# Five of eleven down-projection chunks as seven block products, their weight sums on GpSimd, and the splits at the stage ends placed otherwise

## The chip, the cores and the metric

The kernel runs on one core of a Trainium2 chip. The number that counts is the device time of one execution in microseconds (us). A core has a matrix engine (TensorE, PE in the rows; its weight loads are PEld), a vector engine (VectorE, DVE), an engine for activations and copies (ScalarE, ACT), a general engine (GpSimd, POOL) and an engine that issues transfers (SyncE, SP). Each works through its own program in order and waits on semaphores of the others. Matmuls write to PSUM, eight banks of 128x512 numbers; everything else lies in SBUF.

## The reference

Two layers, each with a feed-forward network, a token mixer and a second feed-forward network, on 256 tokens of 1024 numbers, all in fp32:

```python
def swiglu(h, w_gate_up, w_down):
    gu = h @ w_gate_up                      # 1024 -> 2 * 2816
    g, u = jnp.split(gu, 2, axis=-1)
    return (jax.nn.silu(g) * u) @ w_down    # 2816 -> 1024

for l in range(2):
    x = x + 0.5 * rms_norm(swiglu(rms_norm(x, ffn1_pre[l]), ...), ffn1_post[l])
    x = x + rms_norm(hybrid_mixer(rms_norm(x, mix_pre[l]), ...), mix_post[l])
    x = x + 0.5 * rms_norm(swiglu(rms_norm(x, ffn2_pre[l]), ...), ffn2_post[l])
```

The change touches the product with `w_down`, of which there are four, and the passage from each of them to what follows.

## The kernel before

Every product is made in three passes. A number is split into hi, its value in the matrix engine's fp32r form, and lo, the rest; a product is then hi by hi, hi by lo and lo by hi. Weights come from memory raw, in chunks of 128x2048 (two transfers of 512 KB into two `raw` tiles). ACT casts a raw half to hi, DVE subtracts hi from raw and writes lo. PE uses both.

**Feeding.** `stream` is the list of all chunks in the order of use. `issue` starts a chunk's two transfers and puts the steps of its split into the list `parts`; `part` takes steps off it and writes them into the engines' programs. ACT, DVE and PE keep the order in which they were written (`InOrder`). There are five buffers of hi and of lo (`LOOK + 1`), and six `raw` tiles. `chunk` hands out the next chunk and, through `top_up`, issues as many more as the five buffers hold.

**Block chunks.** In a down projection a chunk is 256 rows of `w_down` by 1024 columns, used with two blocks of 128 tokens. A plain chunk costs 24 matmuls of 512 columns. For the chunks in `FAST` the chunk is taken as two by two blocks of weights (b11, b12, b21, b22, each 128x512) and the activations likewise, and the product is made from seven block products instead of eight (`seven`, with `PRODUCTS`): 7 times three passes, 21 matmuls. The sums of activation blocks that this needs are made in `forms`. The sums of weight blocks are made in place in the raw tiles by four additions of 128x512 (`add`, lines 162 to 172), on DVE. A block chunk so has seven blocks to split and occupies two of the five buffers (`t` with b11, b21, b22; `t2` with four sums). Its steps are, in the order of `parts`: hi of b11; hi of b21 and b22; lo of b11; two additions; hi of the first two sums; lo of b21 and b22; two additions; hi of the last two sums; lo of the four sums. Additions overwrite what earlier steps read, and the last hi needs all four.

**A down projection.** `DOWN` is the order of its eleven chunks. Seven block products use seven PSUM banks; after the last block chunk, `combine` adds the extra banks into the four output banks (DVE, five operations, then three more), while PE does the chunk behind it, the joining chunk. The last three chunks (`TAIL`) are done for the first 128 tokens and then for the second. After the first block `on_block` runs `post` (norm of the result, added to x) and `pre` (norm for the next stage, tile `xn`), PE turns `xn` (`turn`), and then the same for the second block. The next stage begins in `fill` with four chunks.

**Around it.** In the gate and up products before a down projection, ACT copies PSUM banks and DVE adds them (`add_up`), between the splits that `part` puts there. GpSimd has the power of the norms (line 263) and some memsets only.

Of the kernel before, what the change touches and what calls it, by code (L numbers as in the profile page):

```python
# [10 lines left out]
F32 = mybir.dt.float32  # L11
F32R = mybir.dt.float32r
# [4 lines left out]
P = 128  # L17
T = 256
D = 1024
# [14 lines left out]
WARM = 16  # L34
TURN0 = (9, 11)

DOWN = (2, 0, 4, 1, 6, 3, 8, 5, 7, 9, 10)
FAST = (2, 4, 6, 8)


PRODUCTS = (
# [24 lines left out]
@with_exitstack  # L66
def trunk(ctx: ExitStack, tc: tile.TileContext, x, gains, gcol, feat, wgu1, wd1, win, wco, wpg, wpo, wo, wgu2, wd2, out):
    nc = tc.nc
    pe, act, dve = (InOrder(tc, e) for e in (nc.tensor, nc.scalar, nc.vector))
    const = ctx.enter_context(tc.tile_pool(name="const", bufs=1))  # L70
    raws = ctx.enter_context(tc.tile_pool(name="raws", bufs=6))
    whi = ctx.enter_context(tc.tile_pool(name="whi", bufs=LOOK + 1))
# [4 lines left out]
    wide = ctx.enter_context(tc.tile_pool(name="wide", bufs=1))  # L77
# [7 lines left out]
    HALF = (slice(0, 512), slice(512, 1024))  # L85
# [41 lines left out]
    def issue(now=True):  # L127

        i = state["issued"]
        state["issued"] = i + 1  # L130
        name, l, c = stream[i]
        h = CHUNK // 2
        raw = []
        for s in range(2):
            raw.append(raws.tile([P, h], F32, name="raw"))
            nc.sync.dma_start(raw[s], src[name][l, c, :, s * h : (s + 1) * h])
        new = lambda: (whi.tile([P, CHUNK], F32R, name="hi"), wlo.tile([P, CHUNK], F32R, name="lo"))

        def hi(t, at, n, r, off):
            parts.append(lambda: act.copy(t[0][:, at : at + n], raw[r][:, off : off + n]))  # L140

        def lo(t, at, n, r, off):
            parts.append(
                lambda: dve.tensor_tensor(
                    t[1][:, at : at + n], raw[r][:, off : off + n], t[0][:, at : at + n].bitcast(F32), op=ALU.subtract
                )
            )

        t = new()
        if cost(i) == 1:  # L150
            for s in range(2):
                hi(t, s * h, h, s, 0)
                lo(t, s * h, h, s, 0)
            ready[i] = t
        else:


            t2 = new()
            q = h // 2
            b12, b11 = raw[0][:, :q], raw[0][:, q:]  # L160
            b21, b22 = raw[1][:, :q], raw[1][:, q:]
            add = lambda o, x, y, op: parts.append(lambda: dve.tensor_tensor(o, x, y, op=op))
            upper, lower = (t, 0, q, 0, q), (t, q, h, 1, 0)
            hi(*upper)
            hi(*lower)
            lo(*upper)
            add(b11, b11, b12, ALU.subtract)
            add(b12, b22, b12, ALU.subtract)
            hi(t2, 0, h, 0, 0)
            lo(*lower)  # L170
            add(b22, b22, b11, ALU.add)
            add(b21, b21, b22, ALU.subtract)
            hi(t2, h, h, 1, 0)
            lo(t2, 0, h, 0, 0)
            lo(t2, h, h, 1, 0)
            ready[i] = t + t2
        if now:
            part(len(parts))
# [3 lines left out]
    def part(n=1):  # L182
        for _ in range(n):
            if parts:
                parts.pop(0)()
# [70 lines left out]
    def rstd(parts, scale):  # L256

        v0 = small.tile([P, 1], F32, name="v0")
        dve.tensor_scalar(v0, parts[0], scale / D, scale * EPS, op0=ALU.mult, op1=ALU.add)
        v1 = small.tile([P, 1], F32, name="v1")  # L260
        dve.tensor_scalar(v1, parts[1], scale / D, v0, op0=ALU.mult, op1=ALU.add)
        r = small.tile([P, 1], F32, name="r")
        nc.gpsimd.tensor_tensor(r, v1, mhalf, op=ALU.pow)  # L263
        return r

    def sumsq(src_half):
        junk = tmp.tile([P, 512], BF16, name="junk", bufs=1)
        s = small.tile([P, 1], F32, name="ss", bufs=8)
        act.activation(junk, src_half, AF.Square, accum_out=s)
        return s  # L270

    def post(b, banks, gain, scale):

        mul = lambda s: dve.tensor_tensor(banks[s], banks[s], gain[:, HALF[s]], op=ALU.mult)
        ss = sumsq(banks[0])
        mul(0)
        s1 = sumsq(banks[1])
        if b:
            part()
        r = rstd([ss, s1], scale)  # L280
        mul(1)
        for s in range(2):
            dve.scalar_tensor_tensor(
                xs[b][:, HALF[s]], banks[s], r, xs[b][:, HALF[s]], op0=ALU.mult, op1=ALU.add
            )
        if b:
            part()

    def pre(b, gain, r=None):

        if r is None:
            r = rstd([sumsq(xs[b][:, HALF[s]]) for s in range(2)], 1.0)
        xn = wide.tile([P, D], F32, name="xn")
        for s in range(2):
            dve.scalar_tensor_tensor(
                xn[:, HALF[s]], xs[b][:, HALF[s]], r, gain[s], op0=ALU.mult, op1=ALU.mult
            )
        return xn
# [27 lines left out]
    def act_slot(dtype=F32):  # L326

        return acts.tile([P, 2, 512], dtype, name="act", tag="act")
# [4 lines left out]
        split((t[:, :, 0, :], t[:, :, 1, :]), src_ap, 1)  # L333
        return [(t[:, i], t[:, i, 0, :], t[:, i, 1, :]) for i in range(2)]

    def forms(h):


        a = h.rearrange("p i (b t) -> p (i b) t", b=NB)
        sums = tmp.tile([P, 2, T + 2], F32, name="sums", tag="cu", bufs=1)  # L340
        sums = sums.rearrange("p i t -> p (i t)")[:, : 4 * P].rearrange("p (i t) -> p i t", t=P)
        dve.tensor_tensor(sums[:, 0], a[:, 0], a[:, 2], op=ALU.add)
        dve.tensor_tensor(sums[:, 1], sums[:, 0], a[:, 1], op=ALU.subtract)
        dve.tensor_tensor(sums[:, 2], a[:, 1], a[:, 0], op=ALU.subtract)
        dve.tensor_tensor(sums[:, 3], a[:, 3], sums[:, 1], op=ALU.subtract)
        fh, fl = (act_slot(F32R).rearrange("p i (x t) -> p (i x) t", t=P) for _ in range(2))
        split((fh[:, 0:3], fl[:, 0:3]), a[:, 1:4], 1)
        split((fh[:, 3:7], fl[:, 3:7]), sums, 1)
        return fh, fl


    def out_product(name, order, acts_hl, on_block, fast={}):
# [40 lines left out]
        def combine():  # L393

            new = lambda tag: tmp.tile([P, 2, T], F32, name=tag).rearrange("p i t -> p (i t)")
            p1 = new("sil")
            act.copy(p1, extra[1])
            u2 = new("h")
            dve.tensor_tensor(u2, extra[6], p1, op=ALU.add)
            u3 = new("h")  # L400
            dve.tensor_tensor(u3, extra[7], u2, op=ALU.add)
            yield 0, 0
            dve.tensor_tensor(banks[0][0], banks[0][0], u3, op=ALU.add)
            dve.tensor_tensor(u3, u3, extra[5], op=ALU.subtract)
            yield 0, 1
            dve.tensor_tensor(banks[0][1], banks[0][1], u3, op=ALU.add)
            yield 1, 0
            top_up(1)
            dve.tensor_tensor(banks[1][0], banks[1][0], p1, op=ALU.add)
            dve.tensor_tensor(u2, u2, extra[5], op=ALU.subtract)  # L410
            yield 1, 1
            dve.tensor_tensor(banks[1][1], banks[1][1], u2, op=ALU.add)
# [20 lines left out]
        for h in range(2):  # L433
            for c in range(TAIL):
                if len(ws) <= c:
                    ws.append(chunk(name, c))
                for kk in range(2):
                    step(0, h, order[nchunk - TAIL + c], ws[c], kk)
        on_block(0, banks[0])
# [49 lines left out]
    def ffn(l, gu, dn, acts_hl, on_block, gains_):  # L489
        slot = act_slot()  # L490
        tok = [slot[:, f, :] for f in range(2)]

        def take(b, f, p):
            sil = tmp.tile([P, CC], F32, name="sil")
            act.activation(sil, p[:, :CC], AF.Silu)
            dve.tensor_tensor(tok[f][:, b * CC : (b + 1) * CC], p[:, CC:], sil, op=ALU.mult)

        fill(gu, acts_hl, take)
        hs, fast = [], {}
        for f in range(2, NFU):  # L500
            ps = feat_product(gu, acts_hl)
            if f == 2:
                hs += split_pair(turn_back(tok[0]))
            sil = add_up(ps, "sil")
            act.activation(sil, sil, AF.Silu)
            ps = feat_product(gu, acts_hl)
            if f == 2:
                hs += split_pair(turn_back(tok[1]))
            h = add_up(ps, "h")
            dve.tensor_tensor(h, h, sil, op=ALU.mult)  # L510
            if f in FAST:
                fast[f] = forms(h)
                hs += [None, None]
            else:
                hs += split_pair(h)
        gains_()
        out_product(dn, DOWN, hs, on_block, fast)

# [124 lines left out]

    def scaled(b, r):

        xn = wide.tile([P, D], F32, name="xn")
        for h in HALF:
            dve.tensor_scalar(xn[:, h], xs[b][:, h], r, None, op0=ALU.mult)
        return xn
# [114 lines left out]
```

## Time and profile before

| | |
|---|---|
| median of 3 runs | 1172.24 us (1172.19 to 1172.38) |
| profiled execution, its own time | 1171.4 us |
| its span, first to last instruction | 1169.6 us |
| PE busy | 1155.9 us, 99% |
| DVE busy | 914.2 us, 78% |
| ACT busy | 674.1 us, 58% |
| GpSimd busy | 17.3 us, 1% |
| granted TensorE clock, mean | 0.999 |

A profile has a page of totals and several views of the trace behind it. The busy share says how much an engine works, the timeline what ran when and what ended an engine's idle time (in brackets), and the chain of waits which work, followed back from the end, had nothing to spare. A matmul's end is modelled and overlaps the next one's start, so its pace is read from starts. Operations on one engine overlap a little as well; the time after which the next one starts is called the pitch below.

### The profile page before, as it was taken

The numbers are of one execution on the slowest core, as the hardware profiler recorded it, in microseconds if no ns is written. First come the engines' busy times: TensorE is split into PE (matmuls) and PEld (weight loads), VectorE is DVE, ScalarE is ACT, GpSimd is POOL, SyncE is SP. The second block draws the span as 40 slices with busy tenths as digits, with TensorE's granted clock in tenths as the row PEclk, the third lists the DMA queues.
The fourth block names the chain that finished last, engine by engine and source line by source line (L and its number), as shares of the span: only waits on it lengthen the run. The fifth ranks groups of instructions, "written<-read, shape, count | busy, mean of one in ns | idle before, by whom it ended". The sixth has DMA issues, their size and how long they took to land.

```text
span 1169.6 us, 16393 instructions
## 1 busy us (share of the span) xinstructions
PE 1155.9 (99%) x6144; PEld 991.8 (85%) x6144; DVE 914.2 (78%) x1301; ACT 674.1 (58%) x1042; POOL 17.3 (1%) x75
## 2 busy tenths in 40 slices
PE   8999999999999999999999999999999999999997
PEld 5888888888898888888788888878888988888885
DVE  6777798587988767769986769976789786777795
ACT  7565465655565566655565555656556565565561
POOL 0000000000000000000000000000000000000000
PEclk9999999999999999999999999999999999999999
DMA  9665366655466574636765554765565655565361
GB/s 323 223 207 184 108 231 222 230 182 188 157 210 201 173 259 159 201 109 200 267 209 189 182 178 142 244 210 204 183 202 193 191 187 172 201 199 195 126 196 56
DMA packets 62575, 225.00 MB, mean 192 GB/s; under 512 B 7328, under 2 KB 7328, under 8 KB 62496
## 3 DMA queue, kind: packets, MB, share of 16 engines
q1 hardware_dynamic: 62352, 223.96, 57.4%
q8 instruction: 48, 0.79, 0.3%
q14 instruction: 31, 0.25, 0.1%
q10 hardware_dynamic: 144, 0.00, 0.0%
HBM read 222.88 MB, written 1.05 MB: 191 GB/s over the span
## 4 chain that ended last, share of the span: by engine, by line
PE 78%; DVE 14%; DMA 3%; issue 2%; ACT 2%; POOL 0%; DVEq 0%; POOLq 0%; ACTq 0%
PE ps L63 78%; DVE lo L63 8%; DVE raw L63 3%; DMA raw<-in_wd 2%; DMA raw<-in_win 1%; DVE h L63 1%; ACT hi L63 1%; DMA raw<-in_wgu 0%; POOL r L263 0%; ACT junk L63 0%; ACT act L63 0%; DVE ps L63 0%; DVE x L63 0%; DVE xn L63 0%; DVE act L63 0%
## 5 line engine op out<-in xcount | busy, mean ns | idle before, releaser
L63 DVE TENSOR_TENSOR lo<-raw,hi 128x1024 fp32r<-128x1024 f32 (+1 forms) x444 | 522.9, 1201 | 37.1 <-ACT hi L63 36.5
L63 ACT CAST hi<-raw 128x1024 fp32r<-128x1024 f32 (+1 forms) x444 | 448.9, 1034 | 80.5 <-DVE raw L63 55.3
L63 PE MATMUL ps<-xt,hi 128*128 128x512 f32 x1792 | 419.0, 390 | 0.0
L63 PEld LDWEIGHTS ps<-xt,hi 128*128 128x128 f32 x1792 | 332.6, 188 | 66.6
L63 PE MATMUL ps<-hi,act 128*128 128x512 f32 x800 | 235.5, 391 | 0.2
L63 PEld LDWEIGHTS ps<-xt,lo 128*128 128x128 f32 x1792 | 222.7, 192 | 4.4
L63 PE MATMUL ps<-xt,lo 128*128 128x256 f32 x1792 | 225.1, 283 | 0.0
L63 PEld LDWEIGHTS ps<-hi,act 128*128 128x128 f32 x800 | 149.9, 188 | 32.4 <-DVE h L63 1.9
L63 PE MATMUL ps<-lo,act 128*128 128x512 f32 x400 | 140.4, 390 | 0.9 <-DVE lo L63 0.9
L63 DVE TENSOR_TENSOR h<-ps,h 128x256 f32<-128x256 f32 (+1 forms) x140 | 58.6, 430 | 79.4 <-ACT h L63 79.2
L63 ACT COPY h<-ps 128x256 f32<-128x256 f32 x136 | 49.2, 373 | 122.7 <-PE ps L63 122.7
L63 PE MATMUL ps<-hi,xt 128*128 128x512 f32 x384 | 99.8, 394 | 1.0 <-ACT hi L63 0.9
L63 PEld LDWEIGHTS ps<-lo,act 128*128 128x128 f32 x400 | 75.1, 188 | 17.0 <-DVE lo L63 1.7
L63 PEld LDWEIGHTS ps<-hi,xt 128*128 128x128 f32 x384 | 71.1, 188 | 16.0 <-ACT hi L63 1.3
L63 ACT COPY sil<-ps 128x256 f32<-128x256 f32 (+1 forms) x124 | 45.6, 382 | 67.2 <-PE ps L63 67.2
L63 ACT CAST act<-h 128x512 fp32r<-128x512 f32 (+1 forms) x60 | 35.6, 593 | 69.5 <-DVE h L63 69.5
L63 PE MATMUL ps<-act,hi 128*128 128x512 f32 (+1 forms) x320 | 71.4, 369 | 0.0
L63 PEld LDWEIGHTS ps<-act,hi 128*128 128x128 f32 x320 | 57.5, 189 | 9.6
L63 DVE TENSOR_TENSOR sil<-ps,sil 128x256 f32<-128x256 f32 x104 | 40.7, 419 | 26.0 <-ACT sil L63 26.0
L63 PE MATMUL ps<-lo,xt 128*128 128x512 f32 x192 | 53.6, 395 | 1.6 <-DVE lo L63 1.2
L63 DVE TENSOR_TENSOR act<-h,act 128x512 fp32r<-128x512 f32 (+2 forms) x68 | 44.6, 655 | 8.5 <-ACT act L63 8.2
L63 DVE TENSOR_TENSOR raw<-raw 128x512 f32<-128x512 f32 x64 | 44.3, 692 | 2.2
(69 smaller groups left out, 560.6 us busy)
## 6 DMA issues: line engine op xcount, KB each, us to landing
raw<-in_wgu SPq DMA_DIRECT2D x176, 512.0 KB, 4.6
raw<-in_win SPq DMA_DIRECT2D x96, 512.0 KB, 5.1
raw<-in_wd SPq DMA_DIRECT2D x88, 512.0 KB, 4.6
raw<-in_wco SPq DMA_DIRECT2D x16, 512.0 KB, 4.8
raw<-in_wpo SPq DMA_DIRECT2D x16, 512.0 KB, 4.3
raw<-in_wo SPq DMA_DIRECT2D x16, 512.0 KB, 4.4
gain<-in_gains SPq DMA_DIRECT2D x11, 512.0 KB, 4.5
raw<-in_wpg SPq DMA_DIRECT2D x4, 512.0 KB, 3.7
```

The source lines that it names most:

```text
L63: return lambda *a, **kw: self.tc.keep_in_program_order(f(*a, **kw))
```

## The change

`FAST` gets chunk 9 as a fifth member and `DOWN` another order. The four additions of a block chunk are written to GpSimd instead of DVE, in program order. `forms` puts the lo parts of the first block chunk into the tile that `xn` uses later. In the last three chunks of a down projection the next stage's chunks are no longer issued by `chunk`. `post` and `pre` take one step off `parts` each, at places where they had taken none.

```diff
-DOWN = (2, 0, 4, 1, 6, 3, 8, 5, 7, 9, 10)
-FAST = (2, 4, 6, 8)
+DOWN = (2, 4, 0, 6, 8, 1, 9, 3, 5, 7, 10)
+FAST = (2, 4, 6, 8, 9)
...
-            add = lambda o, x, y, op: parts.append(lambda: dve.tensor_tensor(o, x, y, op=op))
+            add = lambda o, x, y, op: parts.append(lambda: pool.tensor_tensor(o, x, y, op=op))
...
         s1 = sumsq(banks[1])
-        if b:
-            part()
+        part()
         r = rstd([ss, s1], scale)
...
         if r is None:
-            r = rstd([sumsq(xs[b][:, HALF[s]]) for s in range(2)], 1.0)
-        xn = wide.tile([P, D], F32, name="xn")
+            ss = [sumsq(xs[b][:, HALF[s]]) for s in range(2)]
+            part(1 - b)
+            r = rstd(ss, 1.0)
+        xn = wide.tile([P, D], F32, name="xn", tag="xn")
...
-        fh, fl = (act_slot(F32R).rearrange("p i (x t) -> p (i x) t", t=P) for _ in range(2))
+        fh = act_slot(F32R).rearrange("p i (x t) -> p (i x) t", t=P)
+        if spare:
+            fl = wide.tile([P, D], F32R, name="fl", tag="xn").rearrange("p (x t) -> p x t", t=P)
+        else:
+            fl = act_slot(F32R).rearrange("p i (x t) -> p (i x) t", t=P)
...
             top_up(1)
+            if state["issued"] == len(stream):
+                part(len(parts))
...
-                    ws.append(chunk(name, c))
+                    ws.append(chunk(name, c, more=not fast))
```

What the programs of the engines hold in consequence is shown at three places. The first is the split of the chunks in the first down projection. On DVE before, `raw<-raw` are the additions and `lo` the differences:

```order
L63 TENSOR_TENSOR lo<-raw,hi 128x512
L63 TENSOR_TENSOR raw<-raw 128x512 x2
L63 TENSOR_TENSOR lo<-raw,hi 128x1024
L63 TENSOR_TENSOR raw<-raw 128x512 x2
L63 TENSOR_TENSOR lo<-raw,hi 128x1024 x4
L63 TENSOR_TENSOR lo<-raw,hi 128x512
L63 TENSOR_TENSOR raw<-raw 128x512 x2
L63 TENSOR_TENSOR lo<-raw,hi 128x1024
L63 TENSOR_TENSOR raw<-raw 128x512 x2
L63 TENSOR_TENSOR lo<-raw,hi 128x1024 x4
```

On GpSimd now, from the start of the program to the norms after the first down projection (`r` is the power of a norm):

```order
L263 TENSOR_TENSOR r<-v_211,mhalf 128x1
L63 TENSOR_TENSOR raw<-raw 128x512 x2
L559 MEMSET cu 128x2x2
L63 TENSOR_TENSOR raw<-raw 128x512 x18
L263 TENSOR_TENSOR r<-v_1784,mhalf 128x1
```

The additions have left DVE, 16 in a down projection, and GpSimd has 20 of them there.

The second place is ACT in the same stage, after the last copy (`h`) out of the gate and up products. The numbers name tiles. Before, with chunks 4 (`raw_1386`, `raw_1388`), 1 (`raw_1434`, `raw_1436`) and 6 (`raw_1469`, `raw_1471`):

```order
L63 COPY h_1373<-ps_1337 128x256
L63 CAST act_1379<-h_1373 128x2x256
L63 CAST hi_1390<-raw_1386 128x512
L63 CAST hi_1390<-raw_1388 128x1024
L63 CAST hi_1392<-raw_1386 128x1024
L63 CAST hi_1392<-raw_1388 128x1024
L63 CAST hi_1438<-raw_1434 128x1024
L63 CAST hi_1438<-raw_1436 128x1024
L63 CAST hi_1473<-raw_1469 128x512
```

Now, with chunks 4 (`raw_1339`, `raw_1341`), 0 (`raw_1404`, `raw_1406`) and 6 (`raw_1442`, `raw_1444`):

```order
L63 COPY h_1379<-ps_1338 128x256
L63 CAST hi_1343<-raw_1339 128x512
L63 CAST act_1386<-h_1379 128x2x256
L63 CAST hi_1343<-raw_1341 128x1024
L63 CAST hi_1345<-raw_1339 128x1024
L63 CAST hi_1345<-raw_1341 128x1024
L63 CAST hi_1408<-raw_1404 128x1024
L63 CAST hi_1408<-raw_1406 128x1024
L63 CAST hi_1446<-raw_1442 128x512
L63 CAST hi_1446<-raw_1444 128x1024
L63 CAST hi_1448<-raw_1442 128x1024
L63 CAST hi_1448<-raw_1444 128x1024
```

Chunk 4 is begun at the same place of ACT's program, but it is now the second chunk that PE uses and not the third. The program goes on with chunk 8, another block chunk. The casts of a block chunk to its second tile (`hi_1345`, `hi_1448`) read the sums and stand ahead of all that ACT does next.

The third place is DVE at the end of the first down projection, from the last step of `combine` to the first norm of the tokens' first block:

```order
 L63 TENSOR_TENSOR ps<-ps,h 128x512
-L63 TENSOR_TENSOR lo<-raw,hi 128x1024 x4
-L63 TENSOR_TENSOR ps<-ps,gain 128x512
-L63 TENSOR_SCALAR v_1770<-ss 128x1
-L63 TENSOR_SCALAR v_1772<-ss,v_1770 128x1
+L63 TENSOR_TENSOR lo<-raw,hi 128x1024 x2
+L63 TENSOR_TENSOR ps<-ps,gain 128x512
+L63 TENSOR_SCALAR v_1782<-ss 128x1
+L63 TENSOR_SCALAR v_1784<-ss,v_1782 128x1
```

Two lo of the next stage's second chunk have left this place; behind the last `xn` of the stage, three lo stand instead of two, the first of them the second half of the next stage's third chunk.

## Rows read from the trace of the kernel before

**Rows 1.** The page: span, and each engine's busy time, share, instructions.
```profile
span 1169.6 us, 16393 instructions
PE 1155.9 (99%) x6144; PEld 991.8 (85%) x6144; DVE 914.2 (78%) x1301; ACT 674.1 (58%) x1042; POOL 17.3 (1%) x75
```
**Rows 2.** Chain of waits: shares of the span by engine, tile and line.
```profile
by line: PE ps L63 78.1%; DVE lo L63 7.7%; DVE raw L63 3.1%; issue 2.5%; DMA raw<-in_wd 1.6%; DMA raw<-in_win 0.9%; DVE h L63 0.9%; ACT hi L63 0.8%; DMA raw<-in_wgu 0.5%; POOL r L263 0.4%; ACT junk L63 0.4%; ACT act L63 0.4%; DVE ps L63 0.3
```
**Rows 3.** Timeline of PE, down projections: start, us, operation, [idle before].
```profile
136.07 3.66 PE L63 MATMUL ps<-hi,act 128*128 128x512 f32 x14
...
146.39 3.56 PE L63 MATMUL ps<-hi,act 128*128 128x512 f32 x15
149.79 1.75 PE L63 MATMUL ps<-lo,act 128*128 128x512 f32 x7
...
192.32 0.66 PE L63 MATMUL ps<-ident,xn 128*128 128x128 f32 x4 [0.67 <-DVE xn L63]
...
195.36 1.09 PE L63 MATMUL ps<-hi,xt 128*128 128x512 f32 x4
...
584.54 0.66 PE L63 MATMUL ps<-ident,xn 128*128 128x128 f32 x4 [0.79 <-DVE xn L63]
...
768.24 0.66 PE L63 MATMUL ps<-ident,xn 128*128 128x128 f32 x4 [0.80 <-DVE xn L63]
```
**Rows 4.** Timeline of DVE, splits in the first down projection.
```profile
140.69 0.69 DVE L63 TENSOR_TENSOR act<-h,act 128x512 fp32r<-128x512 f32 x1 [0.69 <-ACT act L63]
141.30 0.68 DVE L63 TENSOR_TENSOR lo<-raw,hi 128x512 fp32r<-128x512 f32 x1
142.02 1.42 DVE L63 TENSOR_TENSOR raw<-raw 128x512 f32<-128x512 f32 x2
...
145.94 5.30 DVE L63 TENSOR_TENSOR lo<-raw,hi 128x1024 fp32r<-128x1024 f32 x5
151.27 1.42 DVE L63 TENSOR_TENSOR raw<-raw 128x512 f32<-128x512 f32 x2
```
**Rows 5.** Timeline of ACT around the start of the first down projection.
```profile
125.42 0.62 ACT L63 CAST hi<-raw 128x512 fp32r<-128x512 f32 x1
...
136.31 1.04 ACT L63 CAST hi<-raw 128x1024 fp32r<-128x1024 f32 x1
137.25 0.64 ACT L63 COPY h<-ps 128x256 f32<-128x256 f32 x2
140.03 0.62 ACT L63 CAST act<-h 128x512 fp32r<-128x512 f32 x1 [2.15 <-DVE h L63]
```
**Rows 6.** GpSimd's groups: count, busy us, mean ns of one, idle before.
```profile
L263 POOL TENSOR_TENSOR r<-v,mhalf 128x1 f32<-128x1 f32 x24 | 13.2, 550 | 720.0 <-DVE v L63 720.0
L577 POOL MEMSET pool<- 128x32 f32 x12 | 1.2, 125 | 65.7 <-DVE h L63 55.8 <-DVE pool L63 9.9
...
masks.py:199 POOL TENSOR_SCALAR_AFFINE_SELECT ident<-ident 128x128 f32<-128x128 f32 x1 | 0.3, 295 | 0.0
masks.py:197 POOL MEMSET ident<- 128x128 f32 x1 | 0.2, 205 | 0.3 <-POOLq L757 0.3
```
**Rows 7.** Timeline of DVE: start of the combining, and the splits behind it.
```profile
171.82 0.69 DVE L63 TENSOR_TENSOR h<-ps,sil 128x512 f32<-128x512 f32 x1 [0.39 <-PE ps L63]
...
175.47 4.62 DVE L63 TENSOR_TENSOR lo<-raw,hi 128x1024 fp32r<-128x1024 f32 x4
```
**Rows 8.** Timeline of DVE at the end of the first down projection.
```profile
182.01 4.62 DVE L63 TENSOR_TENSOR lo<-raw,hi 128x1024 fp32r<-128x1024 f32 x4
...
187.53 0.69 DVE L63 TENSOR_TENSOR ps<-ps,gain 128x512 f32<-128x512 f32 x1
...
201.79 1.41 DVE L63 SCALAR_TENSOR_TENSOR xn<-x,r,gain 128x512 f32<-128x512 f32 x2 [0.73 <-POOL r L263]
```
**Rows 9.** Timeline of GpSimd, the first norm after that projection.
```profile
187.70 0.55 POOL L263 TENSOR_TENSOR r<-v,mhalf 128x1 f32<-128x1 f32 x1 [68.67 <-DVE v L63]
```

More of the change, by code (lines that the diff above doesn't have):

```diff
@@ L68, in trunk @@
     nc = tc.nc
-    pe, act, dve = (InOrder(tc, e) for e in (nc.tensor, nc.scalar, nc.vector))
+    pe, act, dve, pool = (InOrder(tc, e) for e in (nc.tensor, nc.scalar, nc.vector, nc.gpsimd))
     const = ctx.enter_context(tc.tile_pool(name="const", bufs=1))
@@ L334, in split_pair, with forms @@
         return [(t[:, i], t[:, i, 0, :], t[:, i, 1, :]) for i in range(2)]
-    def forms(h):
+    def forms(h, spare):
         a = h.rearrange("p i (b t) -> p (i b) t", b=NB)
@@ L511, in ffn @@
             if f in FAST:
-                fast[f] = forms(h)
+                fast[f] = forms(h, f == FAST[0])
                 hs += [None, None]
@@ L644, in scaled @@
     def scaled(b, r):
-        xn = wide.tile([P, D], F32, name="xn")
+        xn = wide.tile([P, D], F32, name="xn", tag="xn")
         for h in HALF:
```

## The prediction

> **What bounds the kernel now.** I read the totals first: PE is busy 1155.9 of 1169.6 us [rows 1]. The chain of waits gives 78.1% to matmuls and most of the rest to DVE's lo and to the additions on raw tiles [rows 2]; in the down projections the chain lies on the splits, so there PE and the feeding are nearly level. PE's timeline tells how level. It starts the first down projection at 136.07, fifteen matmuls take 149.79 - 146.39 = 3.40 us, so the pace is 0.2267 us, and the only idle time shown at this stage is 0.67 us before the first turn of xn, 0.79 and 0.80 in the next two such stages [rows 3]. DVE there repeats every 151.27 - 142.02 = 9.25 us for a block chunk and a plain one [rows 4], PE needs 45 x 0.2267 = 10.2. Before, then, DVE has a tenth to spare, and matmuls are what can be saved.
>
> **The change, part by part.**
>
> *Matmuls.* One chunk of 24 becomes one of 21, in four projections: 12 x 0.2267 = 2.7 us less.
>
> *Price of an addition.* DVE took 0.71 us each, 1.42 for two [rows 4]. GpSimd has no such row. Its memset goes from 125 ns for 32 numbers to 205 for 128: about 0.10 us fixed and 0.83 ns a number, for writing alone. The select on 128, which also reads one tile, takes 295, that is 0.70 ns a number more [rows 6]. Two reads and a write over 512 are 0.10 + 512 x (0.83 + 1.40 ns) = 1.24 us. Bounds: writing alone, 0.53; the select's whole rate for each of two inputs, 1.67. I take 1.24, with a hand-off of 0.04 (ACT's cast ends at 140.65, DVE starts at 140.69 [rows 4, 5]): 1.28 each. The Trainium skill, GPSIMD Engine Reference, "Performance versus the Vector engine", gives 4497 ns for 2048 numbers; a quarter, 1.12 us, would by the counts below take off some 8 us.
>
> *Does DVE still run beside it?* The one row near it: a power on GpSimd at 187.70 to 188.25 lies beside a DVE operation of 0.69 us, which is no longer than others of its shape [rows 8, 9]. But that one has one input in PSUM, and the power reads one number. An addition and a lo both read two SBUF tiles. Ends: side by side, no cost; or in turns, each lo wedged into the additions costing its 1.13 us (four take 4.62, the last 1.22 [rows 7]). Rows don't settle it. I take turns as the likelier, since both engines would be streaming three SBUF operands at full length, which that row has on neither; the other end is the first rival. The Trainium skill says the same more sharply: in SBUF — State Buffer, "Who interferes with whom", a DVE instruction with two SBUF inputs contends with a GpSimd instruction that reads SBUF, and the second to issue blocks until the first is done. No row here shows that. By that rule the time is my forecast, without it the first rival.
>
> *The line of a block chunk.* From ACT's first cast on, each step waits for the one before: hi of b11 0.62, lo of b11 0.68, four additions 5.12, the last hi at a pitch of 137.25 - 136.31 = 0.94, two hand-offs: 7.44 us [rows 4, 5]. The next chunk's first cast stands on ACT behind that last hi, which waits for GpSimd. So chunks go through this line one after the other, although no engine is full.
>
> *Entry.* Chunk 4 is now second. Its first cast can't come before the last copies h of the gate and up products; with 2 in the same place as before, its lo of b11 ends as now at 141.98, 5.91 after PE's start [rows 3, 4]. Additions and last cast: 5.91 + 5.12 + 1.04 = 12.07. PE wants that cast after 21 + 10 = 31 matmuls, 7.03. Stall 5.0, four times 20.2. Before, a plain chunk of 5.4 us stood in between.
>
> *Chunks 0, 6, 8, 1, 9.* From the last hi of 4 to that of 9: three lines 22.3; two plain chunks, four casts, 3.8; after a plain chunk lo of b11 waits until DVE has done three lo (1.08 + 3 x 1.13 = 4.47 against 3.48), 1.0 each time; after a block chunk, for one, 0.6. Sum 28.7. PE's way between the same points is 111 matmuls (11 left of 4, then 24, 21, 21, 24 and 10 of 9), 25.2. Stall 3.5, four times 14.1.
>
> *Joining.* DVE comes to the combining after five lo, 1.08 + 5 x 1.13 = 6.73 from the start of 9's last hi; five operations take 175.47 - 171.82 = 3.65 [rows 7]; chunk 7's first lo ends 1.22 later, at 11.6. PE asks for it at 1.04 + 42 matmuls (11 of 9, 24 joining, 6 of chunk 5, one) = 10.6, and for three more halves every three matmuls (0.68) where DVE gives one in 1.13. 1.04 + 3 x 0.45 = 2.4, four times 9.6.
>
> *Stage ends.* Two lo fewer stand before the first norm (4.62 us of four there now [rows 8]), so the three idle times before turns should go: -2.3. But the next stage's third chunk has its second lo behind the last xn, which ends at 203.20: lo ends 1.22 later, 9.0 after the next stage's start at 195.36 [rows 3, 8], while PE asks after 30 matmuls, 6.8. Stall 2.2 in three stages, +6.7. The last stage has nothing behind it.
>
> *Costing nothing:* one more block chunk's forms (about 1.6 us of DVE in gate and up products, where PE shows no idle time and DVE is at 78%); fl in xn's tile, read long before the next xn; the transfers, of which SP sends one half chunk after the gains and not before them. Of GpSimd's queue: the memset of cu now stands between chunk 2's additions and waits for a tile that DVE has left by then; the norms' powers come after the last addition.
>
> *Turns.* Between the additions of a chunk lie its lo of b21 and b22 and its lo of the first two sums: 2 x 1.13. Chunks 4, 6, 8 and 9 are in the line: 9.0 a stage, 36.2 in all. Chunk 2 is split under the gate and up products; were it in the line too, 9 more.
>
> **Sum.** -2.7 + 20.2 + 14.1 + 9.6 - 2.3 + 6.7 = 45.6 side by side; with turns 81.8. On the profiled execution's own 1171.4 that is 1253.2; the median of the runs lies 0.8 above it, so 1254.
>
> **Rivals.**
> - *Side by side.* DVE's lo goes on while GpSimd adds. For it: the row of the power. Against: what that row lacks. 1172.2 + 45.6 = 1218.
> - *Additions as quick as DVE's*, 0.69. The additions in the line (four chunks of four, four times: 64) lose 0.55 each; the stall of chunks 6 to 9 and that of the joining are gone by then and the entry keeps 5.0 - 2.2 = 2.8, so side by side 11.4 + 4.4 - 2.7 = +13, 1185; in turns the line fills again, about 1219. For it: nothing but the memset's 0.83 ns. Against: the select.
> - *Faster.* Additions at the lower bound, 0.53, side by side: a line of 4.6 is under PE's 4.76 for a block chunk, and the entry stall ends if chunk 4 begins the 1.7 us earlier that the plain chunk's missing split allows. Then -2.7 - 2.3 decide, if the last xn also comes 2.2 us earlier: 1167. The point is an addition of some 0.55 us; with the xn stall it is 1174. Against: the select already passes that rate with one input.
> - *Additions at 1.67, in turns:* 64 x 0.43 more, 1282.
>
> **How the numbers follow.** Forecast 0.45, its own range 1240 to 1268 (additions of 1.1 to 1.3, chunk 2 out of or in the line); side by side 0.35; as quick as DVE's 0.10; faster 0.05; slow additions 0.05. A range of 1203 to 1268 leaves out the last two and most of the quick case, 0.17. About 0.2% is what can be told from no change. Slower by more takes everything but the faster case and a little: 0.93; that case splits with its xn stall, 0.04 faster, 0.03 within.
>
> **What would show it.** GpSimd rows `raw<-raw` 128x512: 1.2 us or not, 80 of them. Mean of lo 128x1024 in the down projections: near 1.2 means side by side, well above it turns (or longer additions, if GpSimd is the one held). PE idle before matmuls on `hi`, released by ACT, in each down projection: about 8 us side by side, 17 in turns; about 2.4 before `lo` of the last three chunks; about 2.2 in the next stage's third chunk; none before the turns. Chunks 2 and 4 may change the entry: an entry stall without stalls at 6 and 8 would prove the line wrong. The prediction is wrong in sign if GpSimd's additions come out at half a microsecond.

## The result, and the profile after

The changed kernel took 1256.1 us (median of 4 runs, 1255.2 to 1257.8), the kernel before 1172.2 on the same chip: a ratio of 1.0717, 95% interval 1.0702 to 1.0731. The forecast was 1254 in a range of 1203 to 1268, slower with 0.93.

The totals of the page after answer to [rows 1]:

```profile
span 1253.5 us, 16510 instructions
...
PE 1187.3 (95%) x6132; PEld 1000.7 (80%) x6132; DVE 890.5 (71%) x1265; ACT 681.2 (54%) x1054; POOL 156.2 (12%) x155
...
PEclk9999889999999999997999998899999999999789
```

PE has 12 matmuls fewer and is yet busy 31 us longer: the last line, the granted clock in 40 slices of 31 us, falls in four places, and these are the four down projections (the first is slices 5 and 6). The chain of waits, by engine, answers to [rows 2]: additions on GpSimd stand now second after PE.

```profile
PE 70%; POOL 11%; issue 7%; DVE 7%; DMA 2%; ACT 2%; POOLq 0%; DVEq 0%; SPq 0%; ACTq 0%
```

PE's own waits, summed over the execution (us in total, times, longest us):

```profile
PE ps L63 <- ACT hi L63: 40.9, 19, 3.9
PE ps L63 <- DVE lo L63: 10.4, 22, 1.7
PE ps L63 <- DVE sil L63: 4.5, 4, 1.1
PE ps L63 <- DVE h L63: 2.1, 4, 0.5
```

The timeline of PE in the first down projection and behind it (start, us, operation, idle before in brackets) answers to [rows 3]:

```profile
136.28 0.39 PE L63 MATMUL ps<-hi,act 128*128 128x512 f32 x1
...
139.37 0.50 PE L63 MATMUL ps<-hi,act 128*128 128x512 f32 x1 [1.12 <-DVE sil L63]
139.71 0.40 PE L63 MATMUL ps<-hi,fl 128*128 128x512 f32 x1
...
141.09 0.50 PE L63 MATMUL ps<-hi,act 128*128 128x512 f32 x1 [0.52 <-DVE h L63]
...
148.80 1.20 PE L63 MATMUL ps<-hi,act 128*128 128x512 f32 x4 [3.86 <-ACT hi L63]
152.35 2.07 PE L63 MATMUL ps<-hi,act 128*128 128x512 f32 x4 [2.35 <-ACT hi L63]
154.22 2.98 PE L63 MATMUL ps<-lo,act 128*128 128x512 f32 x7
157.03 0.40 PE L63 MATMUL ps<-hi,act 128*128 128x512 f32 x1
...
171.38 1.20 PE L63 MATMUL ps<-hi,act 128*128 128x512 f32 x4 [2.41 <-ACT hi L63]
174.93 2.07 PE L63 MATMUL ps<-hi,act 128*128 128x512 f32 x4 [2.34 <-ACT hi L63]
176.80 3.19 PE L63 MATMUL ps<-lo,act 128*128 128x512 f32 x7
...
181.14 0.39 PE L63 MATMUL ps<-lo,act 128*128 128x512 f32 x1
...
197.98 0.50 PE L63 MATMUL ps<-lo,act 128*128 128x512 f32 x1 [0.35 <-DVE lo L63]
...
212.30 0.66 PE L63 MATMUL ps<-ident,xn 128*128 128x128 f32 x4
...
215.32 1.09 PE L63 MATMUL ps<-hi,xt 128*128 128x512 f32 x4
...
224.23 0.73 PE L63 MATMUL ps<-lo,xt 128*128 128x512 f32 x2 [1.68 <-DVE lo L63]
```

From its first matmul to that of the next stage the projection takes 215.32 - 136.28 = 79.04 us; before it was 195.36 - 136.07 = 59.29 [rows 3]. With the 1.68 in the next stage that is 21.4 more. Four times 19.75 and three times 1.68 (no stage follows the last projection) are 84.0; the spans differ by 83.9. The waits are where the line of a block chunk was expected to put them: at the entry (148.80, 152.35) and at chunk 8 (171.38, 174.93), each before the two pairs of sums. The idle time before the turn (212.30) is gone.

The same line on GpSimd, chunks 4, 6, 8 and 9, as starts and lengths of four additions each:

```profile
144.21 7.01 POOL L63 TENSOR_TENSOR raw<-raw 128x512 f32<-128x512 f32 x4 [7.57 <-DVE lo L63]
156.50 7.18 POOL L63 TENSOR_TENSOR raw<-raw 128x512 f32<-128x512 f32 x4 [5.29 <-DVE lo L63]
166.71 7.09 POOL L63 TENSOR_TENSOR raw<-raw 128x512 f32<-128x512 f32 x4 [3.02 <-DVE lo L63]
179.09 7.17 POOL L63 TENSOR_TENSOR raw<-raw 128x512 f32<-128x512 f32 x4 [5.29 <-DVE lo L63]
```

GpSimd is busy 12% of the span, but in these 42 us it works 28.5, and its idle time is spent waiting for the lo that stands just ahead of it in the line. The chain, piece by piece, shows what the 7.01 consists of (start us, us, what):

```profile
144.21 2.12 POOL raw L63
...
146.40 1.27 POOL raw L63
...
147.75 1.26 POOL raw L63
...
149.09 2.13 POOL raw L63
```

The second and third addition run alone, but for the last 0.2 us of the third. The first lies beside DVE's lo of b21 and b22, the fourth beside the lo of the first two sums, and each of these two additions takes 0.86 longer. DVE's lo hardly grew; its mean was 1.220 us before:

```profile
L63 DVE TENSOR_TENSOR lo<-raw,hi 128x1024 fp32r<-128x1024 f32 x432 | 524.3, 1236 | 149.6 <-ACT hi L63 149.1
```

So of the two signs that the prediction named, a longer lo or longer additions, it is the second: GpSimd is the one that is held.

### The profile page after: what moved, and what is told of

Read it like the earlier page. It is cut to its first block, busy times and chain, and to the rows that moved or that the text cites. A ratio compares the mean times of both kernels' runs of the same rounds, so it can differ in the third digit from the quotient of the medians.

```text
span 1253.5 us, 16510 instructions
## 1 busy us (share of the span) xinstructions
PE 1187.3 (95%) x6132; PEld 1000.7 (80%) x6132; DVE 890.5 (71%) x1265; ACT 681.2 (54%) x1054; POOL 156.2 (12%) x155
## 4 chain that ended last, share of the span: by engine, by line
PE 70%; POOL 11%; issue 7%; DVE 7%; DMA 2%; ACT 2%; POOLq 0%; DVEq 0%; SPq 0%; ACTq 0%
PE ps L63 70%; POOL raw L63 11%; DVE lo L63 4%; DMA raw<-in_wd 1%; ACT hi L63 1%; DVE h L63 1%; DMA raw<-in_wgu 1%; DVE sums L63 0%; POOL r L263 0%; DVE x L63 0%; ACT h L63 0%; DVE xt L63 0%; DVE sil L63 0%; DVE ps L63 0%; ACT act L63 0%
## 5 line engine op out<-in xcount | busy, mean ns | idle before, releaser
L63 DVE TENSOR_TENSOR lo<-raw,hi 128x1024 fp32r<-128x1024 f32 (+1 forms) x452 | 535.7, 1211 | 149.6 <-ACT hi L63 149.1
L63 ACT CAST hi<-raw 128x1024 fp32r<-128x1024 f32 (+1 forms) x452 | 454.6, 1030 | 158.1 <-POOL raw L63 126.8
L63 PE MATMUL ps<-hi,act 128*128 128x512 f32 x764 | 243.5, 411 | 46.6 <-ACT hi L63 39.9
L63 POOL TENSOR_TENSOR raw<-raw 128x512 f32<-128x512 f32 x80 | 139.0, 1738 | 535.9 <-DVE lo L63 531.3
L63 PE MATMUL ps<-lo,act 128*128 128x512 f32 x396 | 148.4, 429 | 4.2 <-DVE lo L63 4.2
L63 PEld LDWEIGHTS ps<-lo,act 128*128 128x128 f32 x396 | 83.0, 210 | 30.1 <-DVE lo L63 11.9
L263 POOL TENSOR_TENSOR r<-v,mhalf 128x1 f32<-128x1 f32 x24 | 13.2, 551 | 328.1 <-DVE v L63 328.1
```

The costliest lines, as they stand in the source:

```text
L63: return lambda *a, **kw: self.tc.keep_in_program_order(f(*a, **kw))
```

## The experiments

The theory: the time is the line of a block chunk, made longer by additions that take 1.26 us where DVE took 0.71 and that can't go on while DVE reads two SBUF tiles. Rivals: the order of the chunks, the fifth chunk or the stage ends make the loss; the access to SBUF alone makes it, whoever waits; a hand-off or a pair of blocks in one tile makes an addition dear.

**What an addition costs.** A kernel of its own; it computes nothing of the reference and only copies x to the output. Engines run one kind of operation alone or beside another.

```diff
+pool.tensor_tensor(v[:, :w], v[:, :w], v[:, 1024 - w :], op=ALU.subtract)    # 8 times, alone or beside:
+dve.tensor_tensor(d[k % 2], s0, s1, op=ALU.subtract)                      # twoin: 128x1024, two SBUF tiles
+dve.tensor_tensor(d[k % 2][:, :512], ps, s1[:, :512], op=ALU.subtract)    # onein: 128x512, one of them in PSUM
+act.copy(c[k % 2], sa)                                                    # besideact
```

> Nothing of the trunk is computed here: x is copied to the output, and beside it stand rows of additions on GpSimd, 128x512 in place, eight each: both inputs in one tile; inputs in two tiles; the same with 128, 256 and 1024 columns; then the first kind beside DVE operations of two SBUF inputs (128x1024), beside DVE operations with one input in PSUM (128x512), and beside ACT casts. Theory (the port): an addition takes 1.27 us alone whatever its tiles, and about 0.9 more beside a DVE operation that reads two SBUF tiles; 1.27 beside the other two. Rival (the tile): the first and fourth additions of a chunk are long because both inputs lie in one tile; then 2.15 alone with one tile, 1.27 with two, and no change beside DVE. Widths by the prediction's price: 128 columns 0.4, 256 0.7, 1024 2.4 us.

The groups of that kernel (count, busy us, mean ns of one, idle before):

```profile
L22 DVE TENSOR_TENSOR d<-src,src 128x1024 fp32r<-128x1024 f32 x14 | 24.5, 1822 | 0.0
L22 POOL TENSOR_TENSOR twoin<-twoin 128x512 f32<-128x512 f32 x8 | 17.1, 2138 | 0.5
L22 DVE TENSOR_TENSOR d<-ps,src 128x512 fp32r<-128x512 f32 x26 | 15.6, 684 | 0.0
...
L22 POOL TENSOR_TENSOR onein<-onein 128x512 f32<-128x512 f32 x8 | 10.1, 1268 | 0.5
L22 POOL TENSOR_TENSOR besideact<-besideact 128x512 f32<-128x512 f32 x8 | 10.1, 1267 | 0.6
L22 POOL TENSOR_TENSOR cross_a<-cross_b,cross_a 128x512 f32<-128x512 f32 x8 | 10.1, 1262 | 0.5
L22 POOL TENSOR_TENSOR same_alone<-same_alone 128x512 f32<-128x512 f32 x8 | 10.1, 1262 | 0.5
L22 DVE TENSOR_TENSOR dvealone<-src,src 128x1024 fp32r<-128x1024 f32 x8 | 9.8, 1224 | 0.2
```

Alone 1.262, whether its inputs lie in one tile or two. Beside DVE with two SBUF inputs it takes 2.138, and DVE's own 1.822 instead of 1.224: both pay. Beside DVE with an input in PSUM, or beside ACT, nobody pays. That is why the power in [rows 9] beside a DVE operation with a PSUM input [rows 8] told nothing against turns. The Trainium skill, SBUF — State Buffer, "Who interferes with whom", states this contention between a two-input DVE instruction and GpSimd; these rows agree: eight additions go by in 17.65 us, 2.2 each, and in the timeline one DVE operation passes with each of them (DVE starts one at 60.35, 62.56 and 64.76, GpSimd at 61.63, 63.84 and 66.03). The pitches of the two alone, 1.34 (from eight in 10.64) and 1.13 [rows 7], make 2.47, so nearly all of it goes in turns. About 0.3 us of a pair overlaps; 0.19 of an addition doesn't grow with its columns (last section), and whether that is the part that overlaps is not shown.

**The additions back on DVE**, everything else as changed.

```diff
-            add = lambda o, x, y, op: parts.append(lambda: pool.tensor_tensor(o, x, y, op=op))
+            add = lambda o, x, y, op: parts.append(lambda: dve.tensor_tensor(o, x, y, op=op))
```

> The changed kernel with the four additions back on DVE; order, five block chunks and stage ends as changed. Theory (the line, priced by the additions): four additions at 0.72 instead of some 7.1 us take about 4.2 us out of each block chunk's line; the entry stall falls to 2 to 3 us, those of chunks 6 to 9 nearly go: 1185 to 1200 us. Rival (the order): two block chunks in a row with five buffers stall whichever engine adds: within 20 us of the changed kernel, 1236 or more. Rival (DVE had to be relieved): DVE, with 5 x 7 us of block chunks, becomes the bound and it is slower than the changed kernel.

1196.8, ratio 1.0204 (1.0188 to 1.0219), as the theory of the line expected. So 59.3 of the 83.9 us go when DVE adds; the rest is there with DVE's additions too.

**The reverse: the kernel before, with its additions on GpSimd and nothing else changed.**

> The kernel before with nothing changed but the engine of the additions: four block chunks, each followed by a plain one. Theory (the line): hi 0.62, lo 0.68, additions 2.2 + 1.3 + 1.3 + 2.2, last hi 0.94, hand-offs 0.1 make 9.1 us, a plain chunk behind it 2.9, 12.0 against PE's 10.2 for the pair: three pairs a stage lose 5 us, the joining about 2, the passage to the first block chunk 1 to 3: +32 to +48, 1204 to 1220. If additions were 1.27 each (no lengthening), the line would be 10.2, level with PE: 1180 to 1192. Rival (the order): without neighbouring block chunks nothing is lost: 1172 to 1176.

1222.1, ratio 1.0421 (1.0404 to 1.0439): +49 with four block chunks in the old order, a little over what was expected. PE's waits there, of which those on `h` and `sil` (banks that DVE has yet to read after the gate and up products) had been in no term:

```profile
PE ps L63 <- ACT hi L63: 10.3, 9, 1.9
PE ps L63 <- DVE h L63: 9.3, 4, 2.3
PE ps L63 <- DVE lo L63: 5.9, 14, 2.2
PE ps L63 <- DVE xn L63: 3.7, 3, 1.2
PE ps L63 <- DVE sil L63: 2.6, 4, 0.7
```

**Additions that nobody waits for**, and then **none at all.** In the first GpSimd adds as in the changed kernel but writes to a tile of its own.

```diff
-            add = lambda o, x, y, op: parts.append(lambda: pool.tensor_tensor(o, x, y, op=op))
+            aside = lambda: tmp.tile([P, 2, PAD + T], F32, name="pool", bufs=3).rearrange("p i t -> p (i t)")[:, :512]
+            add = lambda o, x, y, op: parts.append(lambda: pool.tensor_tensor(aside(), x, y, op=op))
```

In the second this line is:

```diff
+            add = lambda o, x, y, op: parts.append(lambda: None)
```

> The changed kernel with the 80 additions still on GpSimd, reading the same raw tiles, but written to a tile that nobody reads; the casts of the second tile take the raw values, so the block products are not of the sums. No cast waits for GpSimd, while the additions run beside DVE as before. Theory (the line is what costs): only the matmuls saved and the stage ends are left, -2.7 - 2.3 + 6.7: 1172 to 1180 us. Rival (the port costs by holding DVE up): the lo casts stay long and DVE late: 1195 to 1215. In either case the additions that lie beside lo casts stay near 2.1 us.

1197.6, ratio 1.0205 (1.0186 to 1.0224). The theory's number was missed, and the rival's met: though nobody waits for GpSimd, the kernel is 25 us slower than before. In the down projections PE waits for DVE's lo alone (19.6 us over the execution), and the mean of lo in this run is 1.323, not 1.220:

```profile
L63 DVE TENSOR_TENSOR lo<-raw,hi 128x1024 fp32r<-128x1024 f32 x432 | 558.7, 1323 | 34.6 <-ACT hi L63 34.0
```

ACT also waits 53.1 us for transfers into the raw tiles (5.7 before). These transfers start when a raw tile is free, and the queue's own waits name DVE as what frees it, its lo above all, and never GpSimd, so this lateness too leads back to the longer lo. Whether those 25 us came from the access or from the order was open; hence the second.

> The changed kernel without any addition on weight blocks, the casts taking the raw values (the sums of weight blocks are left out). Beside the run whose additions nobody waited for (1197.6) it shows what GpSimd's reading alone costs DVE. Theory, that it is the shared access: DVE then does its splits at 1.13 each, the waits on lo in the down projections go, the late lo of the next stage's third chunk stays (+5): 1172 to 1182. Rival, that those 1197.6 came from the order and the stage ends and not from GpSimd: 1192 to 1199.

1172.0, ratio 1.0003 (0.9993 to 1.0012). No wait is left in the first down projection; one is in the next stage's third chunk. Matmuls, idle before the turns and the late lo of three stages account for it: -2.7 - 2.3 + 1.73 + 2.08 + 1.75 = 0.6, and the interval of the measured 0.1 reaches to 1.4. The runs in a row: order, fifth chunk and ends, without additions, 0; with GpSimd working in SBUF beside DVE, 25.6 more; with its results waited for, another 58.5. These steps are not shown to be parts of the changed kernel's 83.9. Where nobody waits, GpSimd begins as soon as a transfer has landed and so meets other operations of DVE; there DVE pays (lo 1.323), while in the changed kernel lo is 1.236 and the additions pay.

**Half as long.** Each addition on 256 of its 512 columns, at the same places and with the same hand-offs.

```diff
-            add = lambda o, x, y, op: parts.append(lambda: pool.tensor_tensor(o, x, y, op=op))
+            part256 = slice(0, q // 2)
+            add = lambda o, x, y, op: parts.append(
+                lambda: pool.tensor_tensor(o[:, part256], x[:, part256], y[:, part256], op=op)
+            )
```

> The changed kernel with every addition on 256 of its 512 columns (half of each sum of weight blocks is left out). Theory, that the length of an addition in the line of a block chunk sets the time: alone 0.72 for 1.26 (0.54 each), and where it lies beside lo the overlap is shorter too (0.54 to 1.1 each); four in a line of 16 chunks: 27 to 50 less, 1206 to 1229. Rival, that the hand-offs between the engines, not the lengths, set the line: 1245 to 1256.

1195.9, ratio 1.0195 (1.0180 to 1.0211). The lengths decide, not the hand-offs, and they decided more than expected. GpSimd's timeline in that run, four additions each for chunks 4, 6, 8 and 9, to be laid beside the 7.0 to 7.2 above:

```profile
142.35 4.01 POOL L63 TENSOR_TENSOR raw<-raw 128x256 f32<-128x256 f32 x4 [7.57 <-DVE lo L63]
151.66 4.10 POOL L63 TENSOR_TENSOR raw<-raw 128x256 f32<-128x256 f32 x4 [5.29 <-DVE lo L63]
158.78 4.12 POOL L63 TENSOR_TENSOR raw<-raw 128x256 f32<-128x256 f32 x4 [3.03 <-DVE lo L63]
168.19 4.10 POOL L63 TENSOR_TENSOR raw<-raw 128x256 f32<-128x256 f32 x4 [5.30 <-DVE lo L63]
```

3.03 less a chunk makes 48 for 16 chunks, and PE's waits at chunk 2 (4.5 and 2.1 above) are gone, which the expectation had left out: 55 of the 60 measured.

**The order and the fifth chunk alone**, additions on DVE, stage ends of before. Against the kernel before, with `fl` in `xn`'s tile as changed:

```diff
-DOWN = (2, 0, 4, 1, 6, 3, 8, 5, 7, 9, 10)
-FAST = (2, 4, 6, 8)
+DOWN = (2, 4, 0, 6, 8, 1, 9, 3, 5, 7, 10)
+FAST = (2, 4, 6, 8, 9)
```

> Five block chunks in the change's order, additions on DVE, stage ends of before: what the order and the fifth chunk cost alone. Theory: the change with its additions on DVE took 1196.8, of which its ends make +3 (three stalls of 1.74 less 2.3), so 1192 to 1196. Rival, that the ends make most of that loss: 1180 or less. Rival, that the fifth chunk pays once GpSimd and the ends are out of it: below 1172.

1194.6, ratio 1.0189 (1.0175 to 1.0203). The theory holds. With the run without additions this says: the order costs nothing by itself, but in it the additions are on the path, wherever they are made. Even DVE's 0.71 each leave two waits at the entry (1.03 and 1.39 us), which the order of before, with a plain chunk there, did not have. No run has the fifth chunk without the new order, so the two are not told apart.

**The stage ends**: the changed kernel with the old ones, then the kernel before with the new ones.

```diff
-        part()
+        if b:
+            part()
...
-            part(1 - b)
...
-            if state["issued"] == len(stream):
-                part(len(parts))
...
-                    ws.append(chunk(name, c, more=not fast))
+                    ws.append(chunk(name, c))
```

> The changed kernel with the stage ends of before (the steps in post, pre and combine, and the issue of the last three chunks). Theory: the ends are small against the additions; the 1.68 us stall in the next stage's third chunk goes (three times, -5.0), three idle times before turns come back (+2.3): 1253, that is 1249 to 1258. Rival, that the ends let the split run late and so make a good part of the loss: 1240 or less.

1255.9, ratio 1.0712 (1.0697 to 1.0727): within what was expected, but not to be told from the changed kernel (1.0717). The late lo went (waits on lo 7.1 for 10.4), the waits on xn came back (3.7), and those on hi grew from 40.9 to 44.0: what is gained at a stage's end the next line takes.

> The kernel before with the change's stage ends alone. Theory: the idle times before turns go (-2.3), but the next stage's third chunk has a lo behind the last xn (1.7 to 2.2 each, three times, +5.1 to +6.7): 1175 to 1178 against 1173. Rival, that PE has enough ahead with the order of before: the idle goes and no stall comes, 1170 to 1172. Rival, that neither shows: within 0.1%.

1177.1, ratio 1.0037 (1.0025 to 1.0050), +4.8 where -2.3 + 5.1 to 6.7 was expected. PE waits no longer for xn, and for the late lo it waits 1.74, 2.09 and 1.75 us. Behind the 2.09 the granted clock fell to 0.50 (602 to 604), and the four transposes and twelve matmuls that follow (from 599.93 to 604.74) took 4.81 us, in the first stage 3.22 (from 205.98 to 209.20): -2.3 + 5.6 + 1.6 = 4.9. The first of the three waits:

```profile
205.41 0.74 PE L63 MATMUL ps<-lo,xt 128*128 128x512 f32 x2 [1.74 <-DVE lo L63]
```

**An attempt to keep the good half of the ends**, no idle time before the turns, without the late lo: the kernel before with the new ends, but two more steps taken within the first norm, where DVE had idle time. Against the run just told:

```diff
-        part()
+        part(2 - b)
...
-            part(1 - b)
+            part(2 - 2 * b)
```

> The kernel before with the change's stage ends, but after the first block one more step in post and one more in pre, so that the two lo taken from before the norm lie in DVE's idle time within it (1.33 before v and 0.79 in pre, as the run of the ends alone shows), and the next stage's third chunk has its lo as early as in the kernel before. Theory, that idle before the turns and the late lo are two separate costs: both are gone, -1 to -2.3 against before, 1170 to 1171.5. Rival, that the lo in the norm's gaps push xn out as those ahead of it did: 1172 to 1174. Rival, that the third chunk's wait stays: 1175 to 1177.

1186.5, ratio 1.0121 (1.0104 to 1.0137). All three accounts missed. The timelines of DVE and ACT in that run show why:

```profile
187.92 1.04 ACT L63 CAST hi<-raw 128x1024 fp32r<-128x1024 f32 x1
```

```profile
188.99 1.23 DVE L63 TENSOR_TENSOR lo<-raw,hi 128x1024 fp32r<-128x1024 f32 x1 [2.33 <-ACT hi L63]
190.14 0.15 DVE L63 TENSOR_SCALAR v<-ss 128x1 f32<-128x1 f32 x1
```

The cast that this lo needs stands on ACT behind the squares (`junk`), which wait for the same bank as the norm. The lo comes after them, not in the gap before, and the norm's `v` stands behind it. PE waits 4.14 us for xn instead of 0.67. What looked like idle time of one engine was waiting for an event that the inserted work waits for too. No version tried beats the kernel before.

## Why the prediction was right, step by step

- *Price of an addition*: 1.24 was taken, 1.262 measured. That it fits so well is in part luck: 0.10 fixed and 2.23 ns a number were taken, some 0.19 and 2.1 measured, and the two errors nearly cancel.
- *Turns*: taken at 1.13 for each of two lo a chunk, 2.26; the rows give 7.01 to 7.18 for four additions where four alone are 5.05, so 2.0 to 2.1. The likeliest case was chosen for a reason that the measurement confirms (two engines streaming SBUF operands), and that choice is worth 36 of the 82 us.
- *The line*: from the last hi of chunk 4 to that of 9 the forecast had 28.7 + 3 x 2.26 = 35.5; from the end of 4's additions to the end of 9's it is 186.26 - 151.22 = 35.0.
- *Entry*: 5.0 + 2.26 = 7.3 against waits of 3.86 + 2.35 = 6.2.
- *Chunks 0 to 9*: 3.5 + 6.8 = 10.3 against waits of 2.41 + 2.34 = 4.75. The rest is not in waits, so the sign given for turns, 17 us of PE waiting for `hi` in a projection, was missed: 11.0 here, between that and the 8 for side by side. 11 matmuls from 152.35 to 157.03 take 4.68 where 2.49 is the pace, and 15 from 174.93 to 181.14 take 6.21 where 3.40 is. These 5.0 us are PE at the lower clock (0.50 in 152 to 156 and 176 to 180, last section), and they stand where PE would have waited for the line. The size was right because the line sets it; that it would be slow matmuls was not foreseen.
- *Joining*: 2.4 against 0.35 + 3 x 0.17 = 0.9. DVE is as forecast (its first lo of chunk 7 ends 196.71 + 1.22 = 197.9, 11.6 after the start of 9's last hi at 186.29); PE asks 0.7 later, being late by then.
- *Stage ends*: -2.3 held, there is no idle time before the turn. The late lo costs 1.68, not 2.2. Both come out alone with the new ends in the old kernel: no wait before the turns, and 1.74 to 2.09 for the late lo.
- *Not foreseen*: 1.12 and 0.52 us at chunk 2, PE waiting for banks. "Chunk 2 out of the line" was right for its own products and wrong for the copies: its additions last from 129.19 to 136.65, its last cast stands on ACT ahead of the copies of `sil`, its last lo on DVE ahead of the work on `sil`, and the seven products need those banks. Four times 1.64 is 6.6, where the text had nothing in its sum and 9 as an end of the range.

Of 21.4 us a stage these rows give -0.7 (three matmuls) + 1.6 + 6.2 + 4.75 + 5.0 + 0.9 - 0.7 + 1.7 = 18.75. The other 2.6 are mostly a matter of counting. A wait in brackets begins at the modelled end of the matmul before, 0.39 behind its start, where the pace would have put the next start at 0.227. Taken from starts, the ten waits of this projection are 15.6 us and not 13.5, and the matmul after each takes 0.1 longer (0.34 from 139.37 to the next, for 0.227).

The mechanism held: a line of splits that waits for GpSimd, made longer by turns. That the sum came within 2 us is partly luck: a stage's entry was some 1 us and its joining 1.5 us too dear in it, and chunk 2, which had no place in the sum, brought 1.6.

The weak place was the weight of the side-by-side rival (0.35). What it had for it, one row with a PSUM operand, was no evidence, as the bench showed. One sum among the rivals is off: with additions of 0.53 the entry keeps 5.0 - 2.8 = 2.2 us, and beginning 1.7 earlier leaves 0.5, some 2 us in four projections, so *Faster* would have been 1169 and not 1167. The forecast doesn't rest on it.

## What to carry to other kernels

Work moved to an idle engine is priced by its longest chain, not by the engine's busy share: an engine at 12% can set the end when each of its results is waited for. Before moving a two-input operation to GpSimd, list what DVE does meanwhile: if it reads two SBUF tiles, the two go in turns, and here that cost 25.6 us even where nobody waited for the result. Before filling a gap in one engine, ask which event ends the gap, and whether the filling waits for it as well.

## What the runs showed of the hardware

- *TensorE's granted clock fell at the waits.* Granted clock in stretches of 4 us of the changed kernel (the stretch and its length, busy us of PE, PEld, DVE, ACT, POOL, then the clock, the DMA share, GB/s):

```profile
144.00:148.00 4.00, 0.94 (x4) 0.42 (x3) 1.21 (x2) 0.30 (x1) 3.64 (x3) 1.00 0.00 0
148.00:152.00 4.00, 1.20 (x4) 0.67 (x4) 1.32 (x1) 1.50 (x2) 3.14 (x2) 0.75 0.21 63
152.00:156.00 4.00, 3.65 (x9) 2.88 (x10) 3.67 (x4) 3.65 (x5) 0.00 (x0) 0.50 0.53 185
156.00:160.00 4.00, 4.00 (x17) 3.24 (x16) 1.56 (x2) 0.00 (x0) 3.42 (x2) 0.90 0.62 193
...
176.00:180.00 4.00, 4.00 (x11) 3.13 (x10) 4.00 (x5) 2.23 (x3) 0.91 (x1) 0.50 0.68 181
```

  0.50 is the lower of its two levels, 1.2 GHz. In the changed kernel the slow matmuls stand where PE would have waited for the line; in the attempt at the stage ends nothing hides them: after the 4.14 us wait the two turns and what lies between them took 202.91 - 197.50 = 5.41 us, for 195.36 - 192.32 = 3.04 before [rows 3]. There the wait cost more than its length. It isn't the length alone: with waits of 1.03 and 1.39 us the run with five chunks on DVE fell to 0.50 (148 to 150), and the changed kernel with DVE additions, with 1.04 and 1.39 at the same place, stayed at 1.00.
- *Turns hold back even a tiny operation.* In the bench, GpSimd's addition of 128x1 took 0.19 us alone and 1.04 and 1.17 beside DVE with two SBUF inputs.
- *An addition's size*: 128 columns 0.455, 256 0.724, 512 1.262, 1024 2.339 us: 2.1 ns a number and some 0.19 fixed.
